# Attention scores of two layers: sub-heads in pairs in the two halves of the partitions, no block diagonal of keys

## The chip, the core and the metric

The kernel runs on one core of a Trainium2 chip. The core has a matrix engine (PE, whose weight loads are listed as PEld), a vector engine (DVE), an activation engine (ACT), a general engine (POOL) and a queue that issues transfers (SP). Each takes its instructions in a fixed order, and they wait for one another by semaphores. PE writes its results into PSUM, eight banks of 512 float32 columns on 128 partitions; DVE and ACT read them there. The metric is the device time of one execution in microseconds, smaller being better.

## What is computed

A trunk of two layers works on 256 tokens of width 1024. Layer A is causal differential attention of 8 heads, each with two sub-heads of width 64; layer B is dilated attention with 16 heads in each of three groups (dilation 1, 4 and 16). A squared-ReLU MLP follows each. Of the reference the parts that matter here are the two places where scores are made:

```python
def diff_attention(h, w_qkv, ...):            # layer A: H = 8 heads, c = 2 sub-heads, D = 64
    ...
        s = jnp.einsum('bqhcd,bkhcd->bhcqk', q_blk, k[:, :n_k]).astype(f32) * scale
        s = jnp.where(kpos[None, :] <= qpos[:, None], s, -jnp.inf)
        p = jax.nn.softmax(s, axis=-1)
        a = p[:, :, 0] - lam * p[:, :, 1]
    ...

def dilated_group_attention(q, k, v, window, dilation):   # layer B: 16 heads x 3 groups, D = 64
    ...
    s = jnp.einsum('znqhd,znkhd->znhqk', qb, kb).astype(jnp.float32) * (D ** -0.5)
    s = jnp.where(valid[None, :, None], s, -jnp.inf)
    m = jnp.max(s, axis=-1, keepdims=True)
    p = jnp.exp(s - m)
    ...

DIL_GROUPS = ((128, 1), (512, 4), (2048, 16))   # (window, dilation)
```

Every product in the kernel is made of three: both operands are split into an exact high and low part (`whi`/`wlo`, `th`/`tl`, `hTh`/`hTl` and so on; a copy on ACT makes the high part, a subtraction on DVE the low one), and high by high, high by low and low by high are added up in PSUM.

## The kernel before

The tokens lie in two tiles of 128. In each layer a loop runs over the heads (layer A, `hd`, 8 times) or over pairs of heads (layer B, `hp`, 8 times). One pass makes the projections with `gemm` (lines 289 to 291, 384 columns wide) and starts a generator, `attn_A` or `attn_B`, that emits this head's attention in stages. Between the halves of the weight chunks `tick()` is called: it has `W.pump()` split the next half chunk of weights (line 82 on ACT, line 83 on DVE, up to four halves ahead, five buffers) and moves each running generator on if its count of ticks is used up. A `yield n` in a generator thus means that n steps of the projections, of 12 products each, stand between two stages. `WAIT_A` and `WAIT_B` hold these counts. The order in which each engine works is set by this, and by a list scheduler that moves single instructions a little. After the last pass the remaining stages run beside the output projection (`OutProj.body`, lines 384 to 386, 512 columns wide).

Layer A: lines 498 to 505 transpose q and k of both sub-heads into one bank (line 501) and split them into `th` and `tl`; sub-head 0 lies on partitions 0 to 63, sub-head 1 on 64 to 127. For each sub-head in turn `scores` (lines 341 to 343) then makes three products of 256 columns and three of 128, all with 64 rows.

Layer B: six sub-heads belong to a pair of heads, two of each group. Those of group 0 are transposed together (line 600) and give per head and token block three products of 64 rows and 256 columns by `scores`. Those of groups 1 and 2 of one head are transposed by `both(hh)` (line 583) into `q2` (128 rows, one group above the other) and into `kd`, a tile of keys in block-diagonal form whose other blocks are zero (set once by the memset at line 710); lines 616, 618 and 620 then make three products of 128 rows and 256 columns, which hold the scores of both groups side by side. Each of `both`'s calls has three ACT instructions (lines 585 and 588) and three on DVE (589 and 592). The scores of one head and block fill one bank. The mask and the row maximum are line 351 on DVE, the exponential is line 629 and the scaling by the denominator line 634, both on ACT. `kd` has one buffer, so the second head's `both(1)` comes after the first head's products. Then come the transposes of the probabilities (line 645), their split (`ph`, `pl`, line 337 and 338), and the products with v (lines 658 and 659).

Of the kernel before, what the change touches and what calls it, by code (L numbers as in the profile page):

```python
# [10 lines left out]
F32 = mybir.dt.float32  # L11
# [5 lines left out]
P = 128  # L17
# [85 lines left out]
def trunk(ctx, tc, a):  # L103
# [71 lines left out]
    tabA = hpool.tile([P, NT, 2, 4, HD], F32, name="tabA", tag="tabA")  # L175
    tabB = const.tile([P, 2, NT, 2, 5, HD], F32, name="tabB")
# [8 lines left out]
    def tables_B(ghead, rope):  # L185
        # gains of groups 1 2 0 1 2: a pair's sub-heads take the first three, then the last three
        for t in range(NT):
            for i in range(2):
                for e, g, n in ((0, 1, 2), (2, 0, 3)):
                    nc.gpsimd.tensor_tensor(  # L190
                        tabB[:, i, t, :, e:e + n, :], rope[:, t, :, None, :].to_broadcast([P, 2, n, HD]),
                        ghead[:, None, G * i + g:G * i + g + n, :].to_broadcast([P, 2, n, HD]), op=ALU.mult)
# [45 lines left out]
    def rms(ssx, name, square):  # L238
        """per token tile 1/mean square, or 1/rms and then EPS * mean square, from the four half sums"""
# [12 lines left out]
    def make_hT(x, n, outs):  # L252
        """K tiles of half n of the gained, transposed activations; outs: list of (gain index, hi, lo)"""
# [25 lines left out]
    def gemm_half(pss, h, key, j, i, n):  # L279
        """both token tiles of pss[t][:, :n] += h.T @ w over the two K tiles of half i of chunk j"""  # L280
# [91 lines left out]
    class OutProj:  # L372
        """x += o @ w"""
# [32 lines left out]
    class Mlp:  # L406
# [24 lines left out]
        def first(self, i):  # L431
            """chunk 0, K tiles of half i"""
# [33 lines left out]
        def run(self, rr):  # L466
            """all but the last two chunks' down products"""
# [28 lines left out]
    def attn_A(hd, qr, kr, vt, oh, ol):  # L496
        yield WAIT_A[0]
        tp = wps()
        for i, (tiles, c) in enumerate(((qr, 0), (kr, P))):
            for t in range(NT):  # L500
                nc.tensor.transpose(tp[:, i * S + t * P:i * S + (t + 1) * P], tiles[t][:, c:c + P], ident)
        th = wk.tile([P, 512], F32R, name="th", tag="th")
        tl = wk.tile([P, 512], F32R, name="tl", tag="tl")
        split(th, tl, tp)
# [3 lines left out]
        sm = wk.tile([P, 2, 3 * P], F32, name="smA", tag="sm")  # L508
        for c in range(2):
            rows = slice(c * HD, (c + 1) * HD)  # L510
            sc = wps()
            scores(sc[:, 0:S], th, tl, th, tl, rows, block(1), KALL)
            scores(sc[:, S:S + P], th, tl, th, tl, rows, block(0), slice(S, S + P))
# [9 lines left out]
        # p0 / den0 - lam p1 / den1, times den0 (the norm over the head takes EPS den0^2 instead of EPS)  # L523
# [41 lines left out]
        # from here on the tokens go in two tiles by bit 1 of their number  # L565
# [11 lines left out]
    def attn_B(hp, qr, kr, vts, kd, oh, ol):  # L577
        def both(hh):
            tp = wps()
            for i, tiles in enumerate((qr, kr)):  # L580
                for t in range(NT):
                    c = 4 * hh * HD
                    nc.tensor.transpose(tp[:, i * S + t * P:i * S + (t + 1) * P], tiles[t][:, c:c + P], ident)
            q2 = wk.tile([P, 2, S], F32R, name="q2", tag="q2", bufs=1)
            nc.scalar.activation(q2[:, 0], tp[:, :S], AF.Copy)
            for g in range(2):
                rows = slice(g * HD, (g + 1) * HD)
                nc.scalar.activation(kd[rows, 0, :, g, :], tp[rows, S:].rearrange("p (b k) -> p b k", b=NT), AF.Copy)
            nc.vector.tensor_tensor(q2[:, 1], tp[:, :S], q2[:, 0].bitcast(F32), op=ALU.subtract)
            for g in range(2):  # L590
                rows = slice(g * HD, (g + 1) * HD)
                nc.vector.tensor_tensor(kd[rows, 1, :, g, :], tp[rows, S:].rearrange("p (b k) -> p b k", b=NT),
                                        kd[rows, 0, :, g, :].bitcast(F32), op=ALU.subtract)
            return q2

        yield WAIT_B[0]
        tp = wps()
        for i, tiles in enumerate((qr, kr)):
            for t in range(NT):
                nc.tensor.transpose(tp[:, i * S + t * P:i * S + (t + 1) * P], tiles[t][:, P:2 * P], ident)  # L600
        th = wk.tile([P, 512], F32R, name="th", tag="th")
        tl = wk.tile([P, 512], F32R, name="tl", tag="tl")
# [240 lines left out]
```

## Time and profile before

| what | value |
|---|---|
| three timed runs | 812.39, 812.82 and 814.61 us, median 812.82 |
| profiled execution, span from first to last instruction | 811.9 us |
| PE busy | 794.6 us, 98% of the span |
| DVE busy | 566.7 us, 70% |
| ACT busy | 473.9 us, 58% |
| POOL busy | 182.8 us, 23% |
| HBM read | 129.32 MB |

The page gives no other time of the profiled execution than its span; the median of the timed runs is 0.9 us above it. Layer A's heads run from about 22 to 131 us, the first MLP to about 317 us, layer B's pairs to about 600 us, the output projection to about 630 us and the second MLP to the end. Busy time of PE counts overlapping products once and their ends are modelled, so what PE loses is read from the starts of neighbouring products in the timeline, not from its share.

### The profile page before, as it was taken

To read this page: it belongs to the slowest core of one execution; us is meant where nothing else is said; L and a number is where in the kernel's file an instruction comes from. 1 tells how busy PE (TensorE), PEld (TensorE's weight loads), DVE (VectorE), ACT (ScalarE), POOL (GpSimd) and SP (SyncE) were. 2 spreads that over 40 slices of the span, in tenths; PEclk is the share of its full clock that TensorE was granted. 3 is DMA by queue.
4 is the path that set the end of the run, shared out by engine and by line. 5 is a ranking of instruction groups with operands and counts; after the bars stand their busy time and mean duration, and the time that the engine had idled before them with its cause. 6 is when DMAs were issued, how large, how long until landed. Compare 5 with 4: busy or idle time off the path is not lost.

```text
span 811.9 us, 12783 instructions
## 1 busy us (share of the span) xinstructions
PE 794.6 (98%) x4920; PEld 733.8 (90%) x4920; DVE 566.7 (70%) x953; ACT 473.9 (58%) x853; POOL 182.8 (23%) x172
## 2 busy tenths in 40 slices
PE   6999989999999999999999999999999999999998
PEld 6899967999999998999999999999988999999996
DVE  3998987655555556997879787787976655555553
ACT  5667777444444445666667576666766544444441
POOL 2553441300000000653436253342700000000000
PEclk9999999999999999999999999999999999999999
DMA  8633434454555542454433442443442655545531
GB/s 298 227 137 132 165 132 170 158 203 166 202 190 176 205 161 100 157 194 156 147 126 127 146 149 95 159 143 124 151 156 104 208 168 196 202 165 204 180 132 52
DMA packets 22332, 131.18 MB, mean 162 GB/s; under 512 B 2560, under 2 KB 3328, under 8 KB 13056
## 3 DMA queue, kind: packets, MB, share of 16 engines
q1 hardware_dynamic: 22272, 130.38, 46.0%
q8 instruction: 38, 0.62, 0.3%
q14 instruction: 22, 0.18, 0.1%
HBM read 129.32 MB, written 1.05 MB: 161 GB/s over the span
## 4 chain that ended last, share of the span: by engine, by line
PE 85%; DVE 5%; ACT 5%; issue 2%; POOL 1%; DMA 1%; SPq 0%; DVEq 0%; ACTq 0%; POOLq 0%
PE acc L291 9%; PE acc L290 9%; PE acc L289 9%; PE wps L417 7%; PE wps L416 7%; PE wps L418 7%; PE acc L462 7%; PE acc L463 7%; PE acc L464 7%; PE wps L645 2%; PE acc L384 2%; PE acc L386 2%; PE acc L385 2%; PE wps L659 1%; PE wps L658 1%
## 5 line engine op out<-in xcount | busy, mean ns | idle before, releaser
L83 DVE TENSOR_TENSOR wlo<-raw,whi 128x1024 fp32r<-128x1024 f32 (+1 forms) x272 | 309.5, 1144 | 186.2 <-ACT whi L82 186.0
L82 ACT ACTIVATE whi<-raw 128x1024 fp32r<-128x1024 f32 (+1 forms) x272 | 259.1, 957 | 235.1 <-PE wps L417 98.5
L417 PE MATMUL wps<-hTl,whi 128*128 128x256 f32 x512 | 144.6, 283 | 0.5 <-DVE hTl L271 0.5
L416 PE MATMUL wps<-hTh,whi 128*128 128x256 f32 x512 | 144.3, 283 | 0.7 <-ACT hTh L268 0.7
L418 PE MATMUL wps<-hTh,wlo 128*128 128x256 f32 x512 | 144.6, 283 | 0.0
L325 POOL TENSOR_TENSOR T<-T 128x384 f32<-128x384 f32 (+1 forms) x48 | 44.1, 919 | 334.6 <-DVE ms L243 183.5
L462 PE MATMUL acc<-whi,uh 128*128 128x512 f32 x256 | 100.3, 392 | 0.0
L463 PE MATMUL acc<-wlo,uh 128*128 128x512 f32 x256 | 100.0, 391 | 0.0
L416 PEld LDWEIGHTS wps<-hTh,whi 128*128 128x128 f32 x512 | 97.7, 192 | 2.2 <-ACT hTh L268 1.1
L417 PEld LDWEIGHTS wps<-hTl,whi 128*128 128x128 f32 x512 | 98.0, 192 | 1.9 <-DVE hTl L271 0.7
L464 PE MATMUL acc<-whi,ul 128*128 128x512 f32 x256 | 99.5, 389 | 0.0
L418 PEld LDWEIGHTS wps<-hTh,wlo 128*128 128x128 f32 x512 | 98.1, 192 | 0.0
L289 PE MATMUL acc<-whi,hTh 128*128 128x384 f32 x256 | 88.3, 347 | 0.5 <-ACT hTh L268 0.4
L290 PE MATMUL acc<-wlo,hTh 128*128 128x384 f32 x256 | 86.4, 337 | 1.1 <-DVE wlo L83 1.1
L289 PE MATMUL acc<-whi,hKh 128*128 128x384 f32 x256 | 87.3, 342 | 0.0
L291 PE MATMUL acc<-whi,hTl 128*128 128x384 f32 x256 | 86.2, 337 | 0.0
L291 PE MATMUL acc<-whi,hKl 128*128 128x384 f32 x256 | 85.8, 335 | 0.0
L290 PE MATMUL acc<-wlo,hKh 128*128 128x384 f32 x256 | 85.7, 335 | 0.0
L329 POOL TENSOR_TENSOR f<-ms,half 128x6 f32<-128x6 f32 (+1 forms) x48 | 74.6, 1553 | 3.5 <-DVE ms L320 3.1
L464 PEld LDWEIGHTS acc<-whi,ul 128*128 128x128 f32 x256 | 48.1, 188 | 10.6 <-DVE ul L338 0.4
L462 PEld LDWEIGHTS acc<-whi,uh 128*128 128x128 f32 x256 | 48.2, 188 | 9.9 <-ACT uh L337 0.8
L463 PEld LDWEIGHTS acc<-wlo,uh 128*128 128x128 f32 x256 | 48.2, 188 | 8.7
(130 smaller groups left out, 1363.3 us busy)
## 6 DMA issues: line engine op xcount, KB each, us to landing
raw<-in_wB SPq DMA_DIRECT2D x48, 768.0 KB, 4.3
raw<-in_wup SPq DMA_DIRECT2D x32, 1024.0 KB, 4.8
raw<-in_wdn SPq DMA_DIRECT2D x32, 1024.0 KB, 4.8
raw<-in_wA SPq DMA_DIRECT2D x15, 768.0 KB, 4.6
raw<-in_woA SPq DMA_DIRECT2D x4, 1024.0 KB, 4.8
raw<-in_woB SPq DMA_DIRECT2D x4, 1024.0 KB, 4.8
x<-in_x SPq DMA_DIRECT2D x2, 512.0 KB, 5.1
x<-in_xp SPq DMA_DIRECT2D x1, 1024.0 KB, 7.7
```

What stands on the lines that cost most here:

```text
L82: self.nc.scalar.activation(hi[:, :n], raw, AF.Copy)
L83: self.nc.vector.tensor_tensor(lo[:, :n], raw, hi[:, :n].bitcast(F32), op=ALU.subtract)
L289: nc.tensor.matmul(ps, hh[:, kt, tok], wh[:, c], start=kt == 0, stop=False)
L290: nc.tensor.matmul(ps, hh[:, kt, tok], wl[:, c], start=False, stop=False)
L291: nc.tensor.matmul(ps, hl[:, kt, tok], wh[:, c], start=False, stop=kt == KT - 1)
L329: nc.gpsimd.tensor_tensor(f[:, :nsub], ms[:, :nsub], half[:, :nsub], op=ALU.pow)
L416: nc.tensor.matmul(o, wh[:, c], self.h[0][:, kt, :], start=kt == 0, stop=False)
L417: nc.tensor.matmul(o, wh[:, c], self.h[1][:, kt, :], start=False, stop=False)
L418: nc.tensor.matmul(o, wl[:, c], self.h[0][:, kt, :], start=False, stop=kt == KT - 1)
L462: nc.tensor.matmul(ps, uh[:, tok], dh[:, c], start=first, stop=False)
L463: nc.tensor.matmul(ps, uh[:, tok], dl[:, c], start=False, stop=False)
L464: nc.tensor.matmul(ps, ul[:, tok], dh[:, c], start=False, stop=last)
```

## The change

`scores` is replaced by `scores2`, which makes the scores of two sub-heads at once: the one on partitions 0 to 63 writes into one bank, the one on 64 to 127 into another, and the products alternate between the two; the order of the three parts is low by high, high by low, high by high. `qk_T` holds the transposes and the split; it is called once per head in layer A and three times in a row per pair in layer B (group 0, group 1, group 2; each call has both heads of the pair). `both`, `q2`, `kd` and the memset are gone. The columns of the projections in layer B are put in another order (`SUB`), so that the two heads of a group stand side by side; the table of gains (`tabB`) follows, is made by 12 instead of 8 instructions on POOL, and takes the place in memory where `kd` was. `th` and `tl` get four buffers instead of two. In layer B the scores of both heads are made for one token block at a time, with a yield of two ticks after each block; the softmax of both heads comes after the second block, and one more yield of two ticks stands before the transposes of the probabilities.

```diff
-SUB = ((2, 0, 1), (3, 4, 5))
+SUB = ((2, 0, 4), (3, 1, 5))
...
-    def scores(ps, qh, ql, kh, kl, rows, qs, ks):
-        nc.tensor.matmul(ps, qh[rows, qs], kh[rows, ks], start=True, stop=False)
-        nc.tensor.matmul(ps, qh[rows, qs], kl[rows, ks], start=False, stop=False)
-        nc.tensor.matmul(ps, ql[rows, qs], kh[rows, ks], start=False, stop=True)
+    HALVES = [slice(c * HD, (c + 1) * HD) for c in range(2)]
+    def scores2(pss, t, qs, ks):
+        for i, (q, k) in enumerate(((1, 0), (0, 1), (0, 0))):
+            for rows, ps in zip(HALVES, pss):
+                nc.tensor.matmul(ps, t[q][rows, qs], t[k][rows, ks], start=i == 0, stop=i == 2)
+    def qk_T(qr, kr, c):
+        tp = wps()
+        for i, tiles in enumerate((qr, kr)):
+            for t in range(NT):
+                nc.tensor.transpose(tp[:, i * S + t * P:i * S + (t + 1) * P], tiles[t][:, c[i]:c[i] + P], ident)
+        th = wk.tile([P, 512], F32R, name="th", tag="th", bufs=4)
+        tl = wk.tile([P, 512], F32R, name="tl", tag="tl", bufs=4)
+        split(th, tl, tp)
+        return th, tl
...
     def attn_A(hd, qr, kr, vt, oh, ol):
...
+        scs = [wps(), wps()]
+        scores2([sc[:, 0:S] for sc in scs], T, block(1), KALL)
+        scores2([sc[:, S:S + P] for sc in scs], T, block(0), slice(S, S + P))
...
+    def attn_B(hp, qr, kr, vts, oh, ol):
         yield WAIT_B[0]
+        T0, T1, T2 = [qk_T(qr, kr, (c, c)) for c in (P, 0, 2 * P)]
         yield WAIT_B[1]
+        for b in range(2):
+            own = slice(S + b * P, S + (b + 1) * P)
+            scs = [wps(), wps()]
+            scores2([sc[:, 0:S] for sc in scs], T0, block(b), KALL)
+            scores2([sc[:, S:S + P] for sc in scs], T1, block(b), own)
+            scores2([sc[:, S + P:] for sc in scs], T2, block(b), own)
+            for hh in range(2):
+                masked(sms[hh][:, b, :], scs[hh], mask[:, 4 * b:4 * b + 4, :].rearrange("p b k -> p (b k)"),
+                       -3e38, mxs[hh][:, b:b + 1])
+            yield WAIT_B[2 + b]
         for hh in range(2):
...
-            sms.append(sm)
-            yield WAIT_B[2 + hh]
+        yield WAIT_B[2]
```

On PE, in the scores of a pair in the middle of layer B, these rows stood in a row before (`th` and `tl` hold group 0 of both heads, `q2` and `kd` groups 1 and 2 of one head; `wps_4776` and `wps_4784` are the banks of block 0 and block 1 of the first head):

```order
L341 MATMUL wps_4776<-th_4695 128x256
L342 MATMUL wps_4776<-tl_4696,th_4695 128x256
L343 MATMUL wps_4776<-th_4695,tl_4696 128x256
L616 MATMUL wps_4776<-kd_1887,q2_4704 128x256
L618 MATMUL wps_4776<-kd_1887,q2_4704 128x256
L620 MATMUL wps_4776<-kd_1887,q2_4704 128x256
L341 MATMUL wps_4784<-th_4695 128x256
```

In their place, with 24 products of the projections between the two blocks, these stand now (`th_4691` is group 0, `th_4700` group 1, `th_4709` group 2; `wps_4797` and `wps_4798` are the banks of the two heads, both for block 0):

```order
L346 MATMUL wps_4797<-th_4691,tl_4692 128x256
L346 MATMUL wps_4798<-th_4691,tl_4692 128x256
L346 MATMUL wps_4797<-tl_4692,th_4691 128x256
L346 MATMUL wps_4798<-tl_4692,th_4691 128x256
L346 MATMUL wps_4797<-th_4691 128x256
L346 MATMUL wps_4798<-th_4691 128x256
L346 MATMUL wps_4797<-th_4700,tl_4701 128x128
L346 MATMUL wps_4798<-th_4700,tl_4701 128x128
L346 MATMUL wps_4797<-tl_4701,th_4700 128x128
L346 MATMUL wps_4798<-tl_4701,th_4700 128x128
L346 MATMUL wps_4797<-th_4700 128x128
L346 MATMUL wps_4798<-th_4700 128x128
```

Six more of 128 columns follow for group 2, so one block has 18 products of 64 rows where a head's two blocks had 12, half of them of 64 and half of 128 rows.

On ACT, the softmax of the same pair stood before as follows (`sm_4775` is the first head, `sm_4848` the second; `whi` are the splits of weights, `sq` the squares of the next projections, `ph` the splits of the first head's transposed probabilities):

```order
L629 ACTIVATE sm_4775,den_4774<-sm_4775,nm_4804 128x512 x2
L82 ACTIVATE whi_4911<-raw_4654 128x768
L634 ACTIVATE sm_4775<-sm_4775,rd_4808 128x512 x2
L312 ACTIVATE sq_4885<-acc_4755 128x384
L312 ACTIVATE sq_4898<-acc_4756 128x384
L82 ACTIVATE whi_4931<-raw_4753 128x768
L629 ACTIVATE sm_4848,den_4847<-sm_4848,nm_4865 128x512 x2
L82 ACTIVATE whi_4964<-raw_4753 128x768
L337 ACTIVATE ph_4936<-wps_4938 128x512
L337 ACTIVATE ph_4936<-wps_4945 128x512
L634 ACTIVATE sm_4848<-sm_4848,rd_4869 128x512 x2
```

Now the same engine has, for the two heads `sm_4795` and `sm_4796`:

```order
L311 ACTIVATE sq_4887<-acc_4775 128x384
L606 ACTIVATE sm_4795,den_4937<-sm_4795,nm_4938 128x512
L311 ACTIVATE sq_4900<-acc_4776 128x384
L82 ACTIVATE whi_4933<-raw_4755 128x768
L606 ACTIVATE sm_4795,den_4937<-sm_4795,nm_4938 128x512
L606 ACTIVATE sm_4796,den_4946<-sm_4796,nm_4947 128x512 x2
L82 ACTIVATE whi_4967<-raw_4755 128x768
L611 ACTIVATE sm_4795<-sm_4795,rd_4942 128x512 x2
L611 ACTIVATE sm_4796<-sm_4796,rd_4951 128x512 x2
L82 ACTIVATE whi_4985<-raw_4835 128x768
L336 ACTIVATE ph_4990<-wps_4992 128x512
```

The first head's scaling has moved behind the exponentials of both heads, and all of it behind the second block's scores.

On ACT, in the last pair, beside the output projection (weights of 1024 columns, `ot` is the copy of a product with v), the end stood before like this:

```order
L629 ACTIVATE sm_6870,den_6869<-sm_6870,nm_6887 128x512 x2
L337 ACTIVATE ph_6914<-wps_6916 128x512
L337 ACTIVATE ph_6914<-wps_6923 128x512
L634 ACTIVATE sm_6870<-sm_6870,rd_6891 128x512 x2
L82 ACTIVATE whi_6984<-raw_6728 128x1024
L661 ACTIVATE ot_6959<-wps_6946 64x256
L337 ACTIVATE ph_6962<-wps_6964 128x512
L337 ACTIVATE ph_6962<-wps_6971 128x512
```

and stands now like this:

```order
L606 ACTIVATE sm_6865,den_6945<-sm_6865,nm_6946 128x512 x2
L606 ACTIVATE sm_6866,den_6954<-sm_6866,nm_6955 128x512
L611 ACTIVATE sm_6865<-sm_6865,rd_6950 128x512 x2
L606 ACTIVATE sm_6866,den_6954<-sm_6866,nm_6955 128x512
L82 ACTIVATE whi_6975<-raw_6740 128x1024
L336 ACTIVATE ph_6980<-wps_6982 128x512
L336 ACTIVATE ph_6980<-wps_6989 128x512
L611 ACTIVATE sm_6866<-sm_6866,rd_6959 128x512 x2
L82 ACTIVATE whi_7002<-raw_6740 128x1024
L336 ACTIVATE ph_7024<-wps_7026 128x512
L82 ACTIVATE whi_7125<-raw_6861 128x1024
L637 ACTIVATE ot_7021<-wps_7008 64x256
```

Both heads' exponentials, scalings and splits of probabilities now stand together behind the last scores.

## Rows read from the trace of the kernel before

**Rows 1.** The page's first line: the span.

```profile
span 811.9 us, 12783 instructions
```

**Rows 2.** Busy time by stretch: layer A's sixth head, layer B, one pair.

```profile
core 0: us, PE busy (x) PEld busy (x) DVE busy (x) ACT busy (x) POOL busy (x), PEclk, DMA share, GB/s
78.40:90.50 12.10, 11.69 (x77) 11.18 (x76) 11.03 (x33) 8.97 (x29) 5.36 (x7) 1.00 0.49 173
...
340.00:600.00 260.00, 260.00 (x1612) 249.20 (x1612) 212.55 (x379) 175.05 (x319) 113.82 (x92) 1.00 0.43 146
...
395.70:431.00 35.30, 35.30 (x223) 33.91 (x222) 28.48 (x53) 23.85 (x44) 14.73 (x13) 1.00 0.39 135
```

**Rows 3.** Timeline of PE, layer B, one head's scores: start, us, line, rows*columns, form.

```profile
569.40 0.34 PE L291 MATMUL acc<-whi,hKl 128*128 128x384 f32 x1
569.66 0.38 PE L341 MATMUL wps<-th 64*128 64x256 f32 x1
569.89 0.28 PE L342 MATMUL wps<-tl,th 64*128 64x256 f32 x1
570.00 0.28 PE L343 MATMUL wps<-th,tl 64*128 64x256 f32 x1
570.22 0.39 PE L616 MATMUL wps<-kd,q 128*128 128x256 f32 x1
570.44 0.28 PE L618 MATMUL wps<-kd,q 128*128 128x256 f32 x1
...
571.78 0.60 PE L583 MATMUL wps<-ident,qn 128*128 128x128 f32 x4
```

**Rows 4.** Timeline of PE, layer A's first head, where sub-head 0 hands over to 1.

```profile
33.90 0.28 PE L343 MATMUL wps<-th,tl 64*128 64x256 f32 x1
33.91 0.38 PE L341 MATMUL wps<-th 64*128 64x256 f32 x2
34.08 0.33 PE L342 MATMUL wps<-tl,th 64*128 64x128 f32 x2
34.13 0.28 PE L342 MATMUL wps<-tl,th 64*128 64x256 f32 x1
34.37 0.22 PE L341 MATMUL wps<-th 64*128 64x128 f32 x1
34.43 0.28 PE L342 MATMUL wps<-tl,th 64*128 64x128 f32 x1
34.54 0.27 PE L343 MATMUL wps<-th,tl 64*128 64x128 f32 x1
34.74 0.44 PE L289 MATMUL acc<-whi,hTh 128*128 128x384 f32 x1
35.02 0.33 PE L290 MATMUL acc<-wlo,hTh 128*128 128x384 f32 x1
```

**Rows 5.** Groups by line and form: count, then busy us, mean ns, idle before.

```profile
L616 PE MATMUL wps<-kd,q 128*128 128x256 f32 x32 | 12.4, 386 | 0.0
L351 DVE CUSTOM_DVE_ANT_0 sm<-wps,mask 128x512 f32<-128x512 f32 x32 | 21.3, 685 | 4.4 <-PE wps L620 4.3
L629 ACT ACTIVATE sm<-sm,nm 128x512 f32<-128x512 f32 x32 | 22.8, 713 | 0.0
L82 ACT ACTIVATE whi<-raw 128x768 fp32r<-128x768 f32 x12 | 10.1, 842 | 5.9 <-PE acc L291 5.9
L82 ACT ACTIVATE whi<-raw 128x1024 fp32r<-128x1024 f32 x5 | 5.3, 1055 | 2.3 <-PE acc L386 2.3
L337 ACT ACTIVATE ph<-wps 128x512 fp32r<-128x512 f32 x4 | 2.2, 595 | 0.1
```

**Rows 6.** Timeline of PE where the last pair's attention ends.

```profile
621.70 0.40 PE L384 MATMUL acc<-whi,oTh 128*128 128x512 f32 x1
621.94 0.39 PE L385 MATMUL acc<-wlo,oTh 128*128 128x512 f32 x1
622.32 0.50 PE L384 MATMUL acc<-whi,oTh 128*128 128x512 f32 x1
```

More of the change, by code (lines that the diff above doesn't have):

```diff
@@ L173, in trunk @@
     nc.scalar.activation(warm, half[:, 0:1], AF.Exp)
-    tabA = hpool.tile([P, NT, 2, 4, HD], F32, name="tabA", tag="tabA")
-    tabB = const.tile([P, 2, NT, 2, 5, HD], F32, name="tabB")
+    tabA = hpool.tile([P, NT, 2, 4, HD], F32, name="tabA", tag="tab")
     def tables_A():
@@ L183, in tables_A, with tables_B @@
                     ghead[:, None, i:i + 1, :].to_broadcast([P, 2, 2, HD]), op=ALU.mult)
-    def tables_B(ghead, rope):
+    def tables_B(tabB, ghead, rope):
         for t in range(NT):
             for i in range(2):
-                for e, g, n in ((0, 1, 2), (2, 0, 3)):
+                for e, g, n in ((0, 1, 2), (2, 0, 1), (3, 2, 2)):
                     nc.gpsimd.tensor_tensor(
                         tabB[:, i, t, :, e:e + n, :], rope[:, t, :, None, :].to_broadcast([P, 2, n, HD]),
-                        ghead[:, None, G * i + g:G * i + g + n, :].to_broadcast([P, 2, n, HD]), op=ALU.mult)
+                        ghead[:, None, G * i + g:G * i + g + 1, :].to_broadcast([P, 2, n, HD]), op=ALU.mult)
     nlam = const.tile([P, 1], F32, name="nlam")
@@ L497, in attn_A @@
         yield WAIT_A[0]
[L498 to L504, printed above, removed]
+        T = qk_T(qr, kr, (0, P))
         yield WAIT_A[1]
@@ L508, in attn_A @@
         sm = wk.tile([P, 2, 3 * P], F32, name="smA", tag="sm")
+        scs = [wps(), wps()]
+        scores2([sc[:, 0:S] for sc in scs], T, block(1), KALL)
+        scores2([sc[:, S:S + P] for sc in scs], T, block(0), slice(S, S + P))
         for c in range(2):
[L510 to L513, printed above, removed]
+            sc = scs[c]
             masked(sm[:, c, 0:S], sc[:, 0:S], mask[:, 8:10, :].rearrange("p b k -> p (b k)"),
@@ L571, in attn_A @@
                                            o.bitcast(F32), op0=ALU.mult, op1=ALU.subtract)
[L577 to L594, printed above, removed]
-        yield WAIT_B[0]
[L597 to L602, printed above, removed]
-        split(th, tl, tp)
-        q2 = both(0)
-        yield WAIT_B[1]
-        sms = []
@@ new lines, in attn_B @@
+    def attn_B(hp, qr, kr, vts, oh, ol):
+        yield WAIT_B[0]
+        T0, T1, T2 = [qk_T(qr, kr, (c, c)) for c in (P, 0, 2 * P)]
+        yield WAIT_B[1]
+        mxs = [small.tile([P, 2], F32, name="mx", tag="mx") for _ in range(2)]
+        sms = [wk.tile([P, 2, 4 * P], F32, name="sm", tag="sm") for _ in range(2)]
+        for b in range(2):
[8 more added lines that the diff above has]
+            yield WAIT_B[2 + b]
@@ L607, in attn_B @@
         for hh in range(2):
-            rows = slice(hh * HD, (hh + 1) * HD)
-            mx = small.tile([P, 2], F32, name="mx", tag="mx")
+            sm = sms[hh]
             den = small.tile([P, 2], F32, name="den", tag="den")
-            sm = wk.tile([P, 2, 4 * P], F32, name="sm", tag="sm")
-            for b in range(2):
-                sc = wps()
-                scores(sc[:, 0:S], th, tl, th, tl, rows, block(b), KALL)
-                s2 = sc[:, S:]
-                nc.tensor.matmul(s2, q2[:, 0, block(b)], kd[:, 0, b].rearrange("p g k -> p (g k)"),
-                                 start=True, stop=False)
-                nc.tensor.matmul(s2, q2[:, 0, block(b)], kd[:, 1, b].rearrange("p g k -> p (g k)"),
-                                 start=False, stop=False)
-                nc.tensor.matmul(s2, q2[:, 1, block(b)], kd[:, 0, b].rearrange("p g k -> p (g k)"),
-                                 start=False, stop=True)
-                masked(sm[:, b, :], sc, mask[:, 4 * b:4 * b + 4, :].rearrange("p b k -> p (b k)"),
-                       -3e38, mx[:, b:b + 1])
@@ L624, in attn_B @@
-            if hh == 0:
-                q2 = both(1)
             nm = small.tile([P, 2], F32, name="nm", tag="nm")
-            nc.vector.tensor_scalar(nm, mx, -(HD ** -0.5), None, op0=ALU.mult)
+            nc.vector.tensor_scalar(nm, mxs[hh], -(HD ** -0.5), None, op0=ALU.mult)
             for b in range(2):
@@ L707, in trunk @@
     nc.sync.dma_start(gr[:, 6:10, :], a["rope"][:, 4:8, :])
-    tables_B(gr[:, 0:6, :], gr[:, 6:10, :].rearrange("p (t c) d -> p t c d", t=NT))
-    kd = hpool.tile([P, 2, NT, 2, P], F32R, name="kd", tag="tabA")
-    nc.gpsimd.memset(kd.bitcast(F32), 0.0)
+    tabB = hpool.tile([P, 2, NT, 2, 5, HD], F32, name="tabB", tag="tab")
+    tables_B(tabB, gr[:, 0:6, :], gr[:, 6:10, :].rearrange("p (t c) d -> p t c d", t=NT))
     mlp.run(rms(ssx, "rM0", True))
@@ L747, in trunk @@
             tick()
-        gens.append(start(attn_B(hp, rows[0], rows[1], vts, kd, oh, ol)))
+        gens.append(start(attn_B(hp, rows[0], rows[1], vts, oh, ol)))
     op = OutProj("oB", oh, ol)
```

## The prediction

> **What bounds the kernel now.** Start with busy time by stretch. In layer B, where most of the change lies, PE is busy for 260.00 of 260.00 us, while DVE has 28.48 and ACT 23.85 us of work in the 35.30 us of a pair [rows 2]. So PE sets the pace there, and time comes off only where PE has less to do or loses less between products. In layer A it is nearly a draw: in the sixth head DVE has 11.03 us of work in 12.10 and PE 11.69 [rows 2], and the long gaps of PE are waits for DVE's split of q and k.
>
> A busy share of 100% hides what PE loses, so read next the starts of neighbouring products in the timeline of one head's scores in layer B [rows 3]. Products of 256 columns that follow their like start 0.11 us apart (569.89 to 570.00), and those of 384 columns 0.17. Wherever the number of rows changes from 128 to 64 or back, two things come on top: the first product of the new kind starts about 0.10 late (569.40 to 569.66 is 0.26 instead of 0.17; 570.00 to 570.22 is 0.22 instead of 0.11), and the second starts 0.22 behind the first instead of 0.11 (569.66 to 569.89, 570.22 to 570.44), since its weights were not loaded ahead. A switch costs 0.20 to 0.21 us. From 569.57, where the last product of the projection is through, to 571.78, where the transposes begin, twelve products take 2.21 us: 12 x 0.115 = 1.38, and four switches, 0.83. Line 616 has 32 products, two to such a section [rows 5], so there are 16 sections; the starts of all of them agree within 0.01 us with these.
>
> Third, the one place where the kernel before hands over from one half of the partitions to the other: layer A, sub-head 0 to 1 [rows 4]. At 33.90 sub-head 0 starts its third product of 256 columns; at 33.91, 0.01 us later, sub-head 1 starts its first. (Rows of one line that overlap are merged, "x2"; the second product of the row at 34.08 also stands by itself, at 34.13.) From there both streams run side by side, 256 columns in the upper half while the lower half does its 128-column ones, each in the rhythm it has alone: 34.13 to 34.37 is two products of 256 columns, 0.12 each, beside the lower half's, and the first 128-column pair is 0.06 apart (34.37 to 34.43), later ones 0.11 (34.43 to 34.54). So two halves with two banks do overlap here, loads included. The way back to 128 rows shows the same price as above: 34.54 to 34.74 is 0.20, and 34.74 to 35.02 is 0.28 instead of 0.17.
>
> **Layer B's scores.** The change turns 2 x 12 products of a pair into 2 x 18 of 64 rows, nine in each half, and leaves two switches to a section instead of four. If the halves overlap as in layer A, one half's nine products set the time: the first late by 0.10; first to second 0.22; two steps of 0.12 to the third and to the first 128-column one; 0.06; four steps of 0.11 (128 columns move in 0.06, but the 0.11 row is the rhythm of a row of loads, so I take it); 0.20 to the projection; 0.11 lost on its next product. That is 0.10 + 0.22 + 0.24 + 0.06 + 0.45 + 0.20 + 0.11 = 1.38, say 1.37 with unrounded starts. Each of the 16 sections saves 2.21 - 1.37 = 0.84 us, together **13.4 us**. Nothing takes the freed time back, as DVE and ACT have 19% and 32% idle in a pair.
>
> Here a row and a page speak of the same thing. Between 33.90 and 34.13 PE starts five products of the two halves (one is merged into the row at 33.91), 0.058 us apart, the last two 0.05, with their weight loads among them [rows 4]; the nine pairs above ask for 0.056 where they have 128 columns. The Trainium skill, "TensorE: Matmul & The Clock Gate", section "Wait — 56ns, not 53.3ns?", says that with hardware decoding off the sequencer spends about 62 ns on a matmul, which then becomes the bound for short ones. By that, an estimate from the page's figure, 18 products would take 1.12 us plus two switches, 1.53 us a section, and layer B would gain 10.9 us in place of 13.4; the trace, which goes down to 0.05, disagrees, and I go by the trace.
>
> **Transposes and splits.** There are twelve transposes per pair as before, now in one row; after the four of line 583 PE goes on without a switch, so a longer row costs nothing. Splits on ACT go from one of `th`, two of `q2` and four of `kd` to three full ones, and likewise on DVE: less work, off the path. They must be done before the first scores; between the last transpose and those PE has 24 products of the projections and 12 with v, 24 x 0.17 + 12 x 0.11 = 5.4 us, while three splits on ACT take 3 x 0.595 [rows 5] and as many on DVE a little more, plus one weight split that is queued ahead. That cover is wide. The memset and four more table instructions are on POOL beside the MLP of layer A: nothing.
>
> **The softmax moved behind both blocks.** Take the start of the second block's last product as zero. PE then has 0.3 + 48 x 0.17 = 8.5 us of projections before it transposes the first head's probabilities, and needs the other block's half of them 0.4 later. On ACT stand ahead of the first scaling two squares (about 0.5 each, estimated from line 629 scaled to 384 columns), four exponentials and two weight splits: from about 1.5 us on, 1.0 + 4 x 0.713 + 2 x 0.842 = 5.5 [rows 5], then the scaling, 0.7: ready at 7.7, the second at 8.4. DVE's two masks, 2 x 0.685 [rows 5], end before the first exponential. So PE doesn't wait, with 0.5 to 0.8 us to spare. I take nothing; if this cover is gone, what comes late is paid 7 or 8 times.
>
> **The last pair.** Here only 24 products of the output projection (0.23 to 0.24 each [rows 6]) follow the last scores, 5.8 us, and the extra yield leaves less work to lie beside the rest. The first head's two scalings (three exponentials ahead of them from 1.9 us on) are ready at 4.8 and 5.5: in time. But then ACT has one more exponential, a weight split of 1.055, two splits of probabilities of 0.595 and two scalings [rows 5]: to 8.5 and 9.9 us, while PE has transposes and six products, to 8.1, then waits off and on, about 0.7 in all. Two more weight splits stand ahead of the second head's last split, about 13 us; PE has some 12 us of work up to there, and waits 1. The last `ot`, sum and split find no product left to hide them, 1 us more. Before, the gap there is 0.38 - 0.24 = 0.14 us [rows 6]. I charge **2.5 us**, between 0 (the scheduler's small moves absorb it) and 4.
>
> **Layer A.** Six pairs of products, 0.10 + 0.22 + 0.24 + 0.06 + 0.11 + 0.31 = 1.04, in place of 1.39 (entry 0.10, 1.18 to the projection, 0.11 after): 0.35 x 8 = 2.8 us of PE's time. But in the sixth head DVE has nearly as much to do as PE [rows 2], and the first product now needs the low part too. I take **1.0**, a little over a third, since time that PE saves there can come back as a wait for DVE; the ends are 0 and 2.8.
>
> **The sum.** The profiled execution spans 811.9 us [rows 1], the median of the runs is 0.9 above: I take the changes off the median. 812.8 - 13.4 - 1.0 + 2.5 = 800.9, forecast **801.0 us**. With every doubtful term good, 812.8 - 13.4 - 2.8 = 796.6. With the last pair at 4 and nothing in layer A, 803.4.
>
> **Rivals.** *The softmax comes late.* ACT's chain has 0.5 to 0.8 us of cover. If DVE's splits of weights stretch it by more (they are mixed into the chain, and the denominators wait in DVE's queue), PE waits before the transposes in each of 8 pairs. At 0.6 us of waiting a pair, 8 x 0.6 = 4.8, and 805.8 to 808.2; from 1.4 us a pair on, nothing is left. For it: before, a whole further section of scores stood between the first head's scores and its transposes, and now none does. Against: the walk above. *The halves don't overlap,* since alternating from product to product is not the long handover of rows 4. Then 18 products stand in a row, 6 x 0.118 + 12 x 0.112 = 2.05, with two switches 2.46 a section, 0.25 more than before, 4.0 us in 16; layer A loses the overlap that it has, about 0.4 x 8 = 3.1; with the last pair 812.8 + 4.0 + 3.1 + 2.5 = 822.4, slower. It decides once a section takes over 2.21 us, that is, if less than a quarter of what can lie side by side (2.46 - 1.37) does. Rows 4 speak against it. *The change does not do what it says:* each half's first product waits for its bank, and the banks are those that the splits of groups 1 and 2 just left; if a bank comes free late, the freed time is spent there, and the kernel stays at 812 to 814. The 5.4 us of cover speaks against it.
>
> **How the numbers follow.** Forecast (796.5 to 804.5): 0.72. Softmax late: 0.15, of which nearly all stays under 811. Halves one after the other: 0.06. No change, by the banks: 0.03. More than all terms, under 796.5: 0.04. A measurement of this kernel can tell about 0.3%, 2.4 us, from no change. Faster by more than that: 0.72 + 0.04 + 0.13 = 0.89; within it 0.04; slower 0.07. The range that leaves out two in ten reaches from 796.5 over half of the late-softmax cases to 808.
>
> **What would show it.** The timeline of layer B should have sections of 18 products whose neighbours start almost together, bank by bank, about 1.3 us from the first to the projection, with no 128-row product inside. A pair should take 33.6 us instead of 35.3. PE's waits should name the scaling (rival one) or the splits `tl` (rival three) if those are right, and the stretch beside the output projection of layer B should show PE waiting for `ph` and `oT` for 2 to 3 us. If neighbours in the two halves start 0.11 apart, rival two is right, and the forecast is wrong from its first term.

## The result and the profile after

| | before | after | ratio |
|---|---|---|---|
| timed with the change first shown | 812.61 us | 801.47 us (800.51 to 802.99) | 0.9861, interval 0.9849 to 0.9874 |
| timed once more, beside experiments | 813.16 us | 801.90 us (801.53 to 802.60) | 0.9858, interval 0.9842 to 0.9874 |

The forecast was 801.0. The change takes 11.2 us off, and the largest term, layer B's scores, came out to 0.01 us a section. Three smaller terms did not (layer A, the last pair, the memset), and they nearly cancel. The execution profiled after is the slowest of its four (802.99).

The page after, the span and the busy times; PE's share hardly moves although it has 96 more instructions, as one overlapping pair counts once:

```profile
span 801.2 us, 12863 instructions
PE 779.8 (97%) x5016; PEld 723.4 (90%) x5016; DVE 559.2 (70%) x921; ACT 461.9 (58%) x821; POOL 178.5 (22%) x175
```

Busy time by stretch after: one pair in layer B, and seven microseconds of the tail. The columns are those of [rows 2]; against its 35.30 a pair now takes 33.60, and PE is busy throughout.

```profile
356.19:389.79 33.60, 33.60 (x234) 32.88 (x234) 27.32 (x48) 21.95 (x39) 15.20 (x14) 1.00 0.41 142
609.00:616.00 7.00, 5.48 (x20) 4.26 (x20) 4.08 (x7) 2.81 (x5) 0.00 (x0) 0.76 0.42 150
```

Timeline of PE after, one token block's section of 18 products, which answers to [rows 3]. "x2" are the products of the two halves, which start within 0.01 us of each other and are merged into one row.

```profile
389.52 0.34 PE L290 MATMUL acc<-whi,hKl 128*128 128x384 f32 x1
389.79 0.39 PE L346 MATMUL wps<-th,tl 64*128 64x256 f32 x2
390.01 0.28 PE L346 MATMUL wps<-tl,th 64*128 64x256 f32 x2
390.13 0.29 PE L346 MATMUL wps<-th 64*128 64x256 f32 x2
390.25 0.22 PE L346 MATMUL wps<-th,tl 64*128 64x128 f32 x2
390.31 0.28 PE L346 MATMUL wps<-tl,th 64*128 64x128 f32 x2
...
390.76 0.28 PE L346 MATMUL wps<-th 64*128 64x128 f32 x2
390.97 0.44 PE L288 MATMUL acc<-whi,hKh 128*128 128x384 f32 x1
391.25 0.34 PE L289 MATMUL acc<-wlo,hKh 128*128 128x384 f32 x1
```

Read the starts: 0.27 from the projection to the first pair (0.10 late), 0.22 to the second, 0.12 and 0.12, 0.06, then 0.11 each, 0.21 to the projection, and 0.28 instead of 0.17 to its next product. From 389.69 to 390.97 that is 1.27, with the last 0.11 it is 1.38; the 16 sections agree within 0.02, the 14 beside the projections of layer B within 0.01.

Waits of PE after: engine, tile, line, releaser, us in total, times, longest. There is none for the scaling (line 611) and none for `tl` in layer B; the four for `tl` are layer A's.

```profile
PE wps L346 <- DVE tl L337: 4.1, 4, 1.9
PE wps L430 <- ACT hTh L267: 1.7, 2, 1.0
PE acc L398 <- ACT oTh L336: 1.5, 1, 1.5
...
PE wps L634 <- ACT ph L336: 0.5, 1, 0.5
```

Marks in the timelines show where the time went. From layer A's last projection to the first MLP it is 37.43 before and 36.44 after; from layer B's first projection to the first product of the second MLP 306.93 and 298.80; the first MLP takes 182.43 and 181.81, the second 180.81 and 180.61.

### The profile page after: what moved, and what is told of

Its sections match the earlier page's. It is cut to its first block, busy times and chain, and to the rows that moved or that the text cites. A ratio compares the mean times of both kernels' runs of the same rounds, so it can differ in the third digit from the quotient of the medians.

```text
span 801.2 us, 12863 instructions
## 1 busy us (share of the span) xinstructions
PE 779.8 (97%) x5016; PEld 723.4 (90%) x5016; DVE 559.2 (70%) x921; ACT 461.9 (58%) x821; POOL 178.5 (22%) x175
## 4 chain that ended last, share of the span: by engine, by line
PE 83%; ACT 6%; DVE 6%; issue 2%; DMA 1%; POOL 1%; SPq 0%; DVEq 0%; ACTq 0%
PE acc L288 9%; PE acc L289 9%; PE acc L290 9%; PE wps L430 8%; PE wps L431 8%; PE wps L432 8%; PE acc L476 7%; PE acc L477 7%; PE acc L478 7%; PE wps L346 2%; DVE wlo L83 2%; PE wps L621 2%; ACT smA L529 2%; ACT whi L82 2%; PE wps L353 1%
## 5 line engine op out<-in xcount | busy, mean ns | idle before, releaser
L328 POOL TENSOR_TENSOR f<-ms,half 128x6 f32<-128x6 f32 (+1 forms) x48 | 69.4, 1446 | 4.1 <-DVE ms L319 3.1
```

The costliest lines, as they stand in the source:

```text
L328: nc.gpsimd.tensor_tensor(f[:, :nsub], ms[:, :nsub], half[:, :nsub], op=ALU.pow)
```

## Does the overlap need products that alternate?

The first experiment kept the change and only reordered each section, all of one half's products before the other's (`parts` holds a section's products, three in layer B and two in layer A, each in three parts; `...` is cut code):

```diff
-        for i, (q, k) in enumerate(((1, 0), (0, 1), (0, 0))):
-            for rows, ps in zip(HALVES, pss):
-                nc.tensor.matmul(ps, ...)
+        for rows, c in zip(HALVES, range(2)):
+            for pss, t, qs, ks in parts:
+                for i, (q, k) in enumerate(((1, 0), (0, 1), (0, 0))):
+                    nc.tensor.matmul(pss[c], ...)
```

> The changed kernel with the products of each section in another order, in both layers: first all of one half's (nine in layer B, six in layer A), then all of the other half's, in place of alternating from product to product. What is computed stays the same, to the same two banks, behind the same waits. Theory (PE can have a product of each half under way, but takes them from one row: it looks a few places ahead, as rows 4 showed for layer A of before, where the second sub-head's 256-column products ran beside the first one's 128-column ones): a section of layer B takes about 1.6 to 1.9 us in place of 1.27 to its end, 16 x 0.3 to 0.6, and the time is 806 to 812. Rival one (strictly one after the other at the handover): about 2.3 us a section, 16 x 1.0 plus what layer A loses, 819 to 822. Rival two (the halves' queues are deep enough for nine products, so that the order does not matter): within 1 us of 801.5.

It took 812.24 us, ratio 0.9993 (0.9984 to 1.0003): the whole gain is gone. A section takes 1.90 in place of 1.27, 16 x 0.63 = 10.1 us. So mixing the halves earns 0.63 of the 0.83 us that a section saves; the other 0.20, 3.2 us in all, is kept here. Waits for `pl` take back 0.2 a pair (a pair takes 35.08) and the tail takes the rest: from layer B's first projection to the second MLP it is 307.94, against 306.93 before. Timeline of PE of that kernel, one section; the names of both halves read alike, so mark the row of 256 columns that begins amid those of 128.

```profile
391.28 0.38 PE L345 MATMUL wps<-th,tl 64*128 64x256 f32 x1
...
391.81 0.27 PE L345 MATMUL wps<-tl,th 64*128 64x128 f32 x1
391.92 0.27 PE L345 MATMUL wps<-th 64*128 64x128 f32 x1
391.93 0.38 PE L345 MATMUL wps<-th,tl 64*128 64x256 f32 x2
...
393.09 0.44 PE L288 MATMUL acc<-whi,hKh 128*128 128x384 f32 x1
```

The upper half's first product, tenth in the row, starts at 391.93 with the lower half's sixth (391.92); "x2" is that the lower half's seventh, which begins in its time, is merged into its row. So four of the lower half's nine run beside the upper half's. In [rows 4] it was the same: the seventh started with the third of six, four left. Rival one (strictly one after the other) falls, and so does rival two (any distance will do).

If a distance of four places is what counts, groups of three must do as well as alternation:

```diff
-        for i, (q, k) in enumerate(((1, 0), (0, 1), (0, 0))):
-            for rows, ps in zip(HALVES, pss):
+        for rows, ps in zip(HALVES, pss):
+            for i, (q, k) in enumerate(((1, 0), (0, 1), (0, 0))):
```

> The changed kernel with the products of a section in groups of three: the three of one bank on the lower half, the three of the other bank on the upper half, then the next group of the lower half, in place of alternating from product to product; in both layers. What is computed stays the same. In the run with all nine of a half in a row the second half's first product started beside the sixth of the first half, so that four of nine lay beside it. Theory (that distance of four places is what counts, however the halves are mixed): the second half's first product starts together with the lower half's first or second, a section takes 1.27 to 1.45 us to its end, the time is 801 to 804. Rival (what counts is that neighbours in the row differ in their half, each handover to the other costing the overlap): 1.6 to 1.9 us a section, as with nine in a row, 807 to 812.

They do: the sections take 1.28, and rows of both halves merge again.

```profile
391.27 0.39 PE L346 MATMUL wps<-th,tl 64*128 64x256 f32 x2
```

But the time was 805.84, not 801 to 804: 3.9 us more than the changed kernel beside it. The sections of scores don't have them; the softmax does, as the rows below show.

## How much cover the softmax has

ACT's row in the changed kernel, timeline of one pair (`sm` in line 606 the exponentials, in 611 the scalings). The section's last products start at 396.32.

```profile
398.64 0.73 ACT L606 ACTIVATE sm<-sm,nm 128x512 f32<-128x512 f32 x1 [0.21 <-DVE nm L604]
...
402.58 0.83 ACT L82 ACTIVATE whi<-raw 128x768 fp32r<-128x768 f32 x1
403.32 2.55 ACT L611 ACTIVATE sm<-sm,rd 128x512 f32<-128x512 f32 x4
```

Four scalings in 2.55 us are 0.64 each, so the first is ready at 403.96, 7.6 us behind the last products; PE begins the transposes 8.6 us behind them:

```profile
404.96 0.49 PE L621 MATMUL wps<-ident,sm 128*128 128x128 f32 x3
```

The forecast said 7.7 and 8.5. About 1 us of cover is thin, and the kernel with groups of three shows it. There the list scheduler gave ACT's row another order, though the edit touches only PE's: the first exponential stands ahead of both squares of the projections, where one square came first, and ACT sits idle for 2.33 us until DVE's `nm` is there. All that stands behind is later: the scaling waits for the denominator's reciprocal, and PE for the scaling. ACT and PE of that kernel:

```profile
400.12 0.72 ACT L606 ACTIVATE sm<-sm,nm 128x512 f32<-128x512 f32 x1 [2.33 <-DVE nm L604]
...
406.05 1.34 ACT L611 ACTIVATE sm<-sm,rd 128x512 f32<-128x512 f32 x2 [0.65 <-DVE rd L609]
```

```profile
406.83 1.05 PE L621 MATMUL wps<-ident,sm 128*128 128x128 f32 x6 [0.21 <-ACT sm L611]
```

The wait there is 0.38 at the first transpose, and three later ones start 0.24 late in all: 0.62 a pair. From section to section the pair takes 34.22 (391.27 to 425.49) in place of 33.60. Pairs like this, 0.5 to 0.8 us longer each, make up the 4 us. So rival one of the prediction is real as a mechanism, with 0.6 us a pair; the changed kernel escapes it by 1 us.

Taking the last yield away in every pair asks the same with 24 products less beside the softmax:

```diff
-            yield WAIT_B[2 + b]
+            if b == 0:
+                yield WAIT_B[2 + b]
```

> The changed kernel without the yield behind the second block's scores in any pair: the softmax is emitted at once, and only 24 products of the projections stand between the last scores and the transposes of the probabilities, as the last yield of two ticks leaves them. What is computed stays the same. Theory (the forecast's reckoning: from the last scores on ACT's chain is ready with the first head's scaling at 7.7 us, and 24 products with their 0.17 are only 4.1 us): PE waits 2 to 3 us in each of eight pairs before line 625's transposes, 7 pairs by 2 to 3 is 14 to 21 us, less the 3 to 5 that the tail gives back: 812 to 818. Rival (the softmax is done much earlier than reckoned, and the extra yield is not needed): no waits in the pairs, and the same 796.5 to 798.5 as with the edit in the last pair alone.

Measured: 804.04 us, ratio 0.9892 (0.9877 to 0.9907), pairs of 34.22 us. My theory fell by a factor of four: PE waits 0.62 a pair, not 2 to 3. ACT's row does not stay as it was. Now the scalings come ahead of the fourth exponential and no weight split stands between (timelines of ACT and PE):

```profile
400.60 1.32 ACT L612 ACTIVATE sm<-sm,rd 128x512 f32<-128x512 f32 x2
401.83 0.71 ACT L607 ACTIVATE sm<-sm,nm 128x512 f32<-128x512 f32 x1
```

```profile
401.36 1.05 PE L622 MATMUL wps<-ident,sm 128*128 128x128 f32 x6 [0.22 <-ACT sm L612]
```

The first scaling is ready at about 401.26, 5.1 us behind the last products (396.16) where it was 7.6 before. The yield does pay, 7 x 0.62 = 4.3 us (the kernel of the next section, which keeps it in seven pairs, is 4.6 faster), but I had priced its absence with an order that the scheduler gives up at once.

## The tail of the last pair

Timeline of PE in the changed kernel, where the last pair ends:

```profile
605.51 0.39 PE L634 MATMUL wps<-ph,v 128*128 128x256 f32 x1 [0.51 <-ACT ph L336]
...
608.23 0.40 PE L400 MATMUL acc<-whi,oTl 128*128 128x512 f32 x1
610.08 0.52 PE L398 MATMUL acc<-whi,oTh 128*128 128x512 f32 x1 [1.45 <-ACT oTh L336]
610.41 0.61 PE L399 MATMUL acc<-wlo,oTh 128*128 128x512 f32 x1
610.82 0.63 PE L398 MATMUL acc<-whi,oTh 128*128 128x512 f32 x1
```

PE loses 0.67 at 604.62 to 605.51, then 1.62 (608.23 to 610.08 is 1.85 in place of 0.23), and after that its products of 512 columns stand 0.41 to 0.43 apart. The granted clock of 609 to 616 is 0.76, and 0.53 in 611 to 614, which is nearly all at the lower of the two levels. I took this for a consequence of the wait, and the extra yield of the last pair for the cause of both:

```diff
-            yield WAIT_B[2 + b]
+            if not (b == 1 and hp == HP - 1):
+                yield WAIT_B[2 + b]
```

> The changed kernel with one edit: in the last of the eight pairs there is no yield behind the second block's scores, so that its softmax is emitted at once, as in the kernel before; the other seven pairs stay. What is computed stays the same. Theory (the extra yield of the last pair is what makes the tail dear: in the changed kernel PE waits 0.7 us at 604.6 and 1.6 us at 608.2 for the splits of probabilities, and behind the second wait the granted clock is 0.76 from 609 to 616, with products of 512 columns 0.43 apart in place of 0.23): both waits shrink to under 0.4 us, the clock of that stretch stays near 1.00, and the time falls by 3 to 5 us, to 796.5 to 798.5. Rival (it is the order of the softmax in itself, both heads' exponentials ahead of the scalings, and not the place of the yield): the waits only move, the clock falls all the same, and the time stays within 1 us of 801.5.

Measured: 799.42 us (798.95 to 800.02), ratio 0.9833 (0.9817 to 0.9849); this beats both kernels (the eight executions of the changed one lie between 800.51 and 802.99). Timeline of PE, and the window that stands above:

```profile
604.21 0.39 PE L635 MATMUL wps<-ph,v 128*128 128x256 f32 x1 [0.72 <-ACT ph L336]
...
608.36 0.50 PE L398 MATMUL acc<-whi,oTh 128*128 128x512 f32 x1
```

```profile
609.00:616.00 7.00, 6.23 (x42) 5.17 (x42) 6.63 (x11) 5.50 (x14) 0.00 (x0) 1.00 0.45 150
```

The long wait is gone (0.15 in place of 1.62); the first one is not, it even grew from 0.67 to 0.89 where I wrote under 0.4; and the clock stays at 1.00. From the last projection to the second MLP it is 37.92 in place of 40.83. Was the clock part of that? The changed kernel, run once more without an edit, tells:

> The changed kernel once more, without an edit, so that the other kernels of this set stand beside it on one chip. Expected: within 1 us of 801.5, a tail from the last projection to the first product of the second MLP of 40.8 us, and a granted clock of about 0.76 from 609 to 616. If the clock in that stretch differs from run to run, the 2.9 us that the kernel without the last yield won there are partly chance.

```profile
610.08 0.51 PE L398 MATMUL acc<-whi,oTh 128*128 128x512 f32 x1 [1.45 <-ACT oTh L336]
610.42 0.40 PE L399 MATMUL acc<-wlo,oTh 128*128 128x512 f32 x1
610.65 0.40 PE L398 MATMUL acc<-whi,oTh 128*128 128x512 f32 x1
```

```profile
609.00:616.00 7.00, 5.08 (x28) 3.92 (x29) 5.52 (x9) 4.20 (x10) 0.00 (x0) 1.00 0.42 150
```

The same two waits to the hundredth, and a clock of 1.00 behind them: the tail of 40.8 and the clock of 0.76 that I expected did not come back. So the 2.9 us of the two profiles were 1.4 of waiting, which belongs to the yield, and 1.5 of clock, which this execution had and the other had not (40.83 against 39.35). Each share rests on one pair of profiles. My theory was half chance, and its 3 to 5 us came out as 2.0 to 2.5: the medians are 801.90 and 799.42, the ratios 0.9858 and 0.9833, and the intervals of the two overlap by a little.

## Layer A

The kernel before with layer A's paired products alone (`scores2` and a `qk_T` in `attn_A`, two buffers as before):

```diff
-            sc = wps()
-            scores(sc[:, 0:S], th, tl, th, tl, rows, block(1), KALL)
-            scores(sc[:, S:S + P], th, tl, th, tl, rows, block(0), slice(S, S + P))
+        scs = [wps(), wps()]
+        scores2([sc[:, 0:S] for sc in scs], T, block(1), KALL)
+        scores2([sc[:, S:S + P] for sc in scs], T, block(0), slice(S, S + P))
```

> The kernel before with only layer A's part of the change: the scores of the two sub-heads are made in pairs with alternating products into two banks, with the same two buffers of th and tl as before; layer B is untouched, with its block diagonal of keys. What is computed stays the same. Theory (the two traces: the first product of the first MLP starts 1.7 us earlier after the change, at 135.95 in place of 137.65, since PE's shorter sections, 0.84 us in place of 1.18, partly come back as waits for the low part tl of DVE): 1.0 to 2.3 us less than before, 810.3 to 811.6. Rival one (the gain in layer A comes from the four buffers of th and tl, not from the paired products): no gain, 812.0 to 813.2. Rival two (nothing comes back, the whole 8 x 0.35 is kept): 2.8 less, 809.8.

Measured: 812.63 us, ratio 0.9993 (0.9983 to 1.0003), 0.6 us by the middle of the interval, which takes in no gain at all. By its median this looks like rival one, the four buffers. Sections do fall from 1.18 to 0.84, but PE now waits 4.1 us for `tl` in the heads (2.0 before), in this kernel as in the changed one:

```profile
PE wps L352 <- DVE tl L338: 4.1, 4, 1.9
```

The run with unmixed halves can't tell: its layer A sections are 1.18 again and its first MLP starts at 136.09 us against 136.04 in the changed kernel run anew, but its granted clock was 1.00 from 104 to 110 us, where the nine other profiles have 0.72 to 0.74. The last stretch of layer A stays at 37.46 here, as in the kernel before, while the traces of the changed kernel have 36.4 to 36.5. That 1.0 us must come from elsewhere. The timeline of POOL before, in layer A's last head, has a line that I had not looked up:

```profile
106.40 0.95 POOL L710 MEMSET kd<- 128x1024 f32 x1
...
109.13 1.99 POOL L329 TENSOR_TENSOR f<-ms,half 128x4 f32<-128x4 f32 x1
111.20 0.99 POOL L331 TENSOR_TENSOR qn<-T,f 128x256 f32<-128x256 f32 x1
```

and PE waits for that `qn` before its last transposes:

```profile
110.78 0.27 PE L501 MATMUL wps<-ident,qn 128*128 128x128 f32 x1
112.25 0.55 PE L501 MATMUL wps<-ident,qn 128*128 128x128 f32 x3 [1.20 <-POOL qn L331]
```

The code has the memset behind layer A, but its buffer is free when the last head's table has been used, and the scheduler sets it ahead of the last two factors. The test is the kernel before with the zeros written by two instructions that need the table `gr`, which comes only when layer A is over:

```diff
-    nc.gpsimd.memset(kd.bitcast(F32), 0.0)
+    for i in range(2):
+        nc.gpsimd.tensor_scalar(kd[:, i]..., gr[:, 0:8, :]..., 0.0, None, op0=ALU.mult)
```

> The kernel before, with one edit: the zeros of the block diagonal are written by two GpSimd instructions that read the table grB (times zero), which comes only when layer A is over, in place of the memset, which stood in GpSimd's row ahead of the last head's factor f and product qn (0.95 us at 106.40, with PE's transposes waiting 1.20 us for qn at 110.78 to 112.25). What is computed stays the same. Theory (the memset that the change removes was on the path in layer A's last head, which the forecast had at nothing): the stretch from layer A's last projection to the first MLP falls from 37.43 to 36.4 us, as in the changed kernel, and the time by 1.0 us, ratio 0.9985 to 0.9990. Rival (the 1.0 us comes from the shorter sections of scores or from the four buffers): no change of that stretch, ratio 1.000.

Measured: 811.62 us, ratio 0.9982 (0.9972 to 0.9992), a gain of 1.5 us, interval 0.7 to 2.3, where 1.0 was expected. The stretch is 36.24, and POOL and PE read:

```profile
106.99 1.01 POOL L329 TENSOR_TENSOR f<-ms,half 128x4 f32<-128x4 f32 x1
108.07 0.85 POOL L331 TENSOR_TENSOR qn<-T,f 128x256 f32<-128x256 f32 x1
```

```profile
109.46 0.60 PE L501 MATMUL wps<-ident,qn 128*128 128x128 f32 x4
```

So the memset, and not the four buffers, was the 1.0 us: this kernel has two buffers and the short stretch. In layer A its removal earned 1.0 to 1.2 us, and the paired products about 0.5, which these runs don't tell from nothing: the same layer A takes 125.0 to 126.7 us, from its first projection to the first MLP, from one profile to another.

## Two switches fewer

Both token blocks in one section of 36 products, four banks, no yield between them, and none behind the last pair's:

```diff
-            yield WAIT_B[2 + b]
+        if hp < HP - 1:
+            yield WAIT_B[2]
```

> The changed kernel with both token blocks' scores in one section of 36 products (four banks) in place of two sections of 18, so that a pair has two switches of row number in place of four, and, as in the run without the last yield, none between the last pair's scores and its softmax. What is computed stays the same. Theory (a switch costs 0.20 us wherever it stands, since neither the drain nor the first load is covered): the pair's period falls by 0.41 from 33.60, 8 x 0.41 = 3.3 us less than without the last yield alone, about 796. Rival one (the eight banks do not allow four for scores beside the transposes and the projections): waits before the section, a period of 33.6 or more, 799 or above. Rival two (the softmax, now one step of 12 products behind what it had between the blocks, is late): a wait before the transposes of the probabilities of up to 0.6 us a pair, as without the yields, 798 to 801.

Measured: 800.46 us (799.22 to 801.64), ratio 0.9837 (0.9820 to 0.9855): not the 796 of the theory, and no better than the kernel without the last yield. The section is nearly as expected. At the seam the step is 0.11, as inside a section, and the next one 0.17 in place of 0.12 (timeline of PE), and 36 products take 2.29 in place of 2 x 1.27; with the product behind it, 0.36 a pair is saved.

```profile
391.66 0.28 PE L346 MATMUL wps<-th 64*128 64x128 f32 x2
391.77 0.33 PE L346 MATMUL wps<-th,tl 64*128 64x256 f32 x2
391.94 0.28 PE L346 MATMUL wps<-tl,th 64*128 64x256 f32 x2
```

But the pair's period stays at 33.66 (357.21 to 559.14 in six), since PE now waits in a place that neither rival named, the low part `pl` of the probabilities:

```profile
406.85 0.39 PE L636 MATMUL wps<-pl,v 128*128 128x256 f32 x1 [0.18 <-DVE pl L337]
```

In this pair 0.34 are lost here and 0.11 at the next product. Whether another count of ticks would keep the 0.36 was not tried.

## Why the prediction was right, and where not

**Layer B's scores: right in every step.** Forecast 2.21 to 1.37 a section and 13.4 us in all; measured 1.38 and 16 x 0.83 = 13.3. The steps read off [rows 3] and [rows 4] came back one by one (0.10, 0.22, 0.12, 0.12, 0.06, 0.11, 0.20, 0.11). Rival two is wrong for the changed kernel, and its price was sound: 2.46 for no overlap, less four products of 0.113 that lie beside the others, is 2.01, and the kernel with unmixed halves took 1.90 + 0.11.

Between 390.31 and 390.76, over four pairs and so eight products, PE starts one every 0.056 us. The 62 ns that the Trainium skill gives for hardware decoding off, in "TensorE: Matmul & The Clock Gate", "Wait — 56ns, not 53.3ns?", would have made a section 1.53, by the prediction's estimate from that figure. It took 1.38, so the trace disagrees with that as a bound here, as the prediction had it; how these kernels were decoded, no run here shows.

**Transposes and splits: right.** No wait for `tl` in layer B, and 33.60 for a pair as forecast. **But "the memset ... nothing" was wrong**, and it is the step with the plainest lesson: I took its place from the code, beside the MLP, and did not look for it in POOL's timeline. It was worth 1.0 to 1.2 us.

**Softmax: right,** term 0, with 1.0 us of cover for 0.5 to 0.8 forecast; the groups of three show that another order on ACT is enough to lose it. The place of the yield earns 4.3 us, against its absence.

**The last pair: right in kind, too small.** Of 13.3 us, 306.93 - 298.80 = 8.1 are left at the second MLP, so the tail cost 5.2 in that profile, and by the other one (317.89 to 615.07, 297.18) 3.5. Forecast 2.5, ends 0 and 4: the first lies outside, the second inside. The wait for `ph` was right (0.7 and 0.67). The end was not: I had 1 us for the second head's split and 1 for the last `ot`, sum and split; it is 1.62 in one piece and then 1.0 for `hTh` before the second MLP, where the kernel before had no wait. The 1.5 us of clock are in one execution and not in the sum.

**Layer A: too large for what it named.** 1.0 from the shorter sections; measured about 0.5, since the waits for DVE's `tl` doubled.

**The sum.** 13.3 + 1.1 (memset) + 0.5 (layer A) - 3.5 (tail) = 11.4, against 11.2 measured; the forecast's was 13.4 + 1.0 - 2.5 = 11.9. Two terms were mis-sized and one was missing, and that they cancel to half a microsecond is luck. The marks of the kernel before and the changed one run anew divide their 11.4 otherwise: layer A 0.9 in place of 1.6, first MLP 0.6, layer B with its tail 9.7, second MLP 0.2. What stays open: the first MLP takes 181.8 to 181.9 us in all seven traces that have the new layer B, and 182.1 to 182.7 in the three others, which none of these runs explains.

## What to carry to other kernels

Products on the two row halves overlap for as long as the second half's stand within about four places of the first half's in PE's row; mix them that finely, in groups of three or one by one; nine in a row lost 0.63 of the 0.83 us that a section had gained, and what lies between three and nine was tried only with the six of layer A. Look up each removed instruction in its engine's timeline before calling it free: the code's place and the scheduler's are two things. And give the last pass of a software pipeline its own waits, since work that hides the softmax seven times is not there the eighth.

## What the runs showed of the hardware

**A reach of four places.** In three orders (six, nine and three products of one half in a row) the other half's first product started with the third, the sixth and the first. The Trainium skill, "TensorE: Matmul & The Clock Gate", section "The mechanism", has products start and end strictly in program order; the trace disagrees on the starts, as the tenth product starts at 391.93 and the seventh to ninth behind it; the ends are modelled in these traces and show nothing here.

**The clock after a wait.** After the same 1.45 us of waiting, behind the same work, the granted clock stood at 0.53 in 611 to 614 in one execution and at 1.00 in another, 1.5 us apart. Nothing in these two traces tells which it will be; a single profile of a tail should not be read to the microsecond.

**POOL beside DVE.** The last `f` of 128x4 took 1.99 us with the memset and 1.01 without it, so the 0.95 us of the memset held `qn` up by about 1.9. The traces show why: it moved this `f` into a weight split of DVE. Timeline of DVE before:

```profile
108.71 1.54 DVE L83 TENSOR_TENSOR wlo<-raw,whi 128x1024 fp32r<-128x1024 f32 x1
```

The `f` began at 109.13, 0.42 us into the split, and ended 0.87 us behind it; without the memset it began 0.25 ahead of one. The only other long `f` of layer A before, 1.73 us at 45.68, began 0.14 into a split and ended 0.88 behind it, and in layer B all nineteen `f` of 128x6 that began 0.5 to 0.8 us into a split ended 1.18 to 1.20 behind it. So the end of the split sets the end of `f`; one that began within 0.02 us of a split's start took its usual 1.01.
